# Decay matrices through a DRAM round trip, and a quota that binds only when tiles are scarce

## The chip, the cores and the metric

The kernel runs on one core of one Trainium2 chip. A core has TensorE (PE in the profile), VectorE (DVE), ScalarE (ACT), GpSimd (POOL), SyncE (SP, which here only issues DMAs) and 16 DMA engines. The metric is the device time of one execution in microseconds; the median of several runs counts.

## The reference

Two layers over 256 tokens of width 1024, in float32. Each layer is a SwiGLU FFN (inner width 2816), a mixer, and a second FFN, each with a DeepNorm residual and LayerNorm. Layer 0's mixer is a hybrid of a gated delta rule (GDN, 8 value heads) and a state space scan (SSD, 16 heads); layer 1's is a sparse attention (NSA). What matters here are the decay matrices of the hybrid:

```python
def decay_matrix(cs):
    n = cs.shape[-1]
    mask = np.tril(np.ones((n, n), dtype=bool))
    return jnp.exp(jnp.where(mask, cs[..., :, None] - cs[..., None, :], -jnp.inf))
...
    g_cum = jnp.cumsum(g, axis=-1)                 # gated_delta_rule, one g per token and head
    decay = decay_matrix(g_cum)
    attn = jnp.einsum('bhncd,bhnsd->bhncs', q, k) * decay
...
    a_cs = jnp.cumsum(adt, axis=-1)                # ssd_scan
    seg = decay_matrix(a_cs)
    y_diag = jnp.einsum('bgcls,bgecls,bcsgep->bclgep', cb, seg, xdt)
```

All g are negative, so the cumulative sums fall along the tokens. The kernel works in blocks of 128 tokens, with 24 heads (8 GDN, 16 SSD) side by side. For a head and a block it needs exp(cum[t] - cum[s]) with s on the partitions and t along the row; entries with t < s are masked away later, by the masks that are multiplied into q-k and C-B products.

## The kernel before, in words

The program is written as a list of operations on virtual tiles (class Plan). `Plan.order` then simulates the engines with a price for each operation and writes out one fixed order for all engines, SP among them; `emit` issues it. Every engine works through its part in that order, and waits where an operand isn't there. So a change to any operation may reorder all the others. A `copy` may be given to ACT or to DVE, whichever that order finds free earlier.

Every activation tensor and every split weight is a tile of 128 x 1024 floats with the tag m4; there are 36 of them. A weight is loaded raw (four buffers, tag raw, on SP's queue) and split into a high and a low part: `whi` (a copy with rounding to fp32r, on ACT or DVE) and `wlo` (the remainder, on DVE). A product takes three fp32r matmuls. Tiles belong to streams: W (split weights), M (mixers), S and Z (SSD and gates), L and G (residuals and FFN products), P and Q (attention). `QUOTAS` bounds how many tiles a stream may hold: W has (12, 24). The first number holds as long as a tile of another stream (L and G excepted) which comes earlier in the program has not been given its memory yet (`pending_before`), the second otherwise. The check stands in `try_alloc` inside `Plan.order`.

The hybrid mixer (`hybrid`) computes the z gate of the GDN, then the small logits, from which g comes (tile g24: 128 tokens x 2 blocks x 24 heads), then k and q with their short convolutions (`gdn_conv`, `conv_tile`). The rest is five generators that `weave` interleaves so that PE always finds work: `delta` (the triangular solve of the GDN), `space` (value and SSD projections), `gate` (the SSD's z gate), `space2` (the SSD scan) and `out_a` (the first half of the output projection).

`decays` is called twice in `delta` (tile DT, one for each block) and four times in `space2` (tile G). A call makes the matrices for eight heads. It works on g split into gh + gl: for four heads at a time POOL writes `bm`, which is g of partition r repeated along t and set to zero where t < r (an affine_select for gh and one for gl); PE multiplies both by `m_gtr`, the matrix that is 1 for r > s, into one PSUM bank, which gives the sum of g over s < r <= t; ACT takes Exp out of PSUM into DT or G. So a call has four selects, four matmuls of 128 x 512 and two Exp. In `delta`, DT is then multiplied with bp and the k-k product into AT (8 DVE steps per block), from which the solve starts; bp comes from the squared norms of k, through a power on POOL. In `space2`, G is multiplied by the C-B product and is the stationary operand of eight matmuls.

Of the kernel before, what the change touches and what calls it, by code (L numbers as in the profile page):

```python
# [9 lines left out]
F32 = mybir.dt.float32  # L10
F32R = mybir.dt.float32r
I32 = mybir.dt.int32
AF = mybir.ActivationFunctionType
OP = mybir.AluOpType
# [14 lines left out]
CAPS = {  # L29
    "raw": (RAW, "SB"), "m4": (M4, "SB"), "x": (2, "SB"),  # L30
    "cv": (3, "SB"),
    "ps": (2, "PSUM"), "mp": (2, "PSUM"), "acc": (4, "PSUM"),
}

# [14 lines left out]
def H3(t, h):  # L49
    return t.rearrange("p (h t) -> p h t", h=h)  # L50
# [26 lines left out]
class V:  # L77
# [59 lines left out]
    def to_broadcast(self, shape):  # L137
        return self._new(("bc", list(shape)), np.broadcast_to(self.ids, shape[1:]))

    def bitcast(self, dt):  # L140
        return self._new(("bit", dt), self.ids, dtype=dt)

    def real(self):
        x = self.t.real
        for s in self.chain:
            if s[0] == "get":
                x = x[s[1]]
            elif s[0] == "re":
                x = x.rearrange(s[1], **s[2])
            elif s[0] == "bc":  # L150
                x = x.to_broadcast(s[1])
            else:
                x = x.bitcast(s[1])
        return x
# [7 lines left out]
class Plan:  # L162
# [152 lines left out]
    def order(self, caps):  # L315
# [43 lines left out]
        def try_alloc(key):  # L359
            q = queues[key]  # L360
            while heads[key] < len(q):
                t = q[heads[key]]
                wait = blocked[key].get(id(t))
                if not wait:
                    return
                fs = free_slots[t.tag]
                if not fs:
                    return
                if t.quota is not None:
                    small, big = t.quota  # L370
                    lim = small if pending_before(t.tag, t.stream, t.order) else big
                    if live[key] >= lim:
                        return
                i = min(range(len(fs)), key=lambda j: fs[j])
                t.slot_free = fs.pop(i)
                live[key] += 1
                heads[key] += 1
                del blocked[key][id(t)]
                granted.append(t)
                for op in wait:  # L380
                    op.alloc.remove(t)
                    op.ready = max(op.ready, t.slot_free)
                    if not op.alloc:
                        release_ready(op)
# [147 lines left out]
class K:  # L532
# [43 lines left out]
    def consts(self):  # L576
# [12 lines left out]
        self.m_le = sel("m_le", OP.is_ge, -1, 1)  # L589
        self.m_lt = sel("m_lt", OP.is_gt, -1, 1)  # L590
        self.m_gt = sel("m_gt", OP.is_gt, 1, -1)
        self.m_gtr = self.one([P, P], "m_gtr", F32R)
        self.copy(self.m_gtr, self.m_gt)
        self.mhalf = self.one([P, 1], "mhalf")
        nc.vector.memset(self.mhalf, -0.5)

# [395 lines left out]
        V.tensor_scalar(dst, dst, 1.0, None, OP.add)  # L992
        V.reciprocal(dst, dst)

    def decays(self, g, dst, stream, bank):

        nc = self.nc
        for q in range(2):
            bm = self.m4(1024, "bm", stream, F32R).rearrange("p (e h t) -> p e h t", e=2, h=4)
            for e in range(2):  # L1000
                nc.gpsimd.affine_select(bm[:, e], g[e][:, q * 4:q * 4 + 4, None].to_broadcast([P, 4, P]),
                                        pattern=[[0, 4], [1, P]], compare_op=OP.is_ge, fill=0.0, base=0,
                                        channel_multiplier=-1)
            ps = self.bank(bank)
            for e in range(2):
                nc.tensor.matmul(ps, self.m_gtr, bm[:, e].rearrange("p h t -> p (h t)"), start=e == 0, stop=e == 1)
            nc.scalar.activation(dst[:, q * 4:q * 4 + 4, :], H3(ps, 4), AF.Exp)

    def z_gate(self, x, w_in, c0, zs):

# [21 lines left out]
    def hybrid(self, x, then):  # L1032
# [66 lines left out]
        V.scalar_tensor_tensor(sp, xs, 0.0, sp, OP.max, OP.add)  # L1099
        g = self.sm([P, 2, 24], "g24")  # L1100
        V.scalar_tensor_tensor(g, sp, -1.0, rate[:, None, :].to_broadcast([P, 2, 24]), OP.mult, OP.mult)
        gh, gl = (self.sm([P, 2, 24], n, dtype=F32R) for n in ("gh", "gl"))
        V.tensor_copy(gh, g)
        V.tensor_tensor(gl, g, gh.bitcast(F32), OP.subtract)
        g2 = [gh, gl]
        pg = self.bank("mp")
        gf = g.rearrange("p b h -> p (b h)")
        for n, m in enumerate((self.m_le, self.m_gt, self.ones)):
            nc.tensor.matmul(pg[:, n * 48:(n + 1) * 48], m, gf, start=True, stop=True)
        E = self.sm([P, 3, 2, 24], "E")  # L1110
        nc.scalar.activation(E.rearrange("p a b h -> p (a b h)"), pg[:, :144], AF.Exp)
        eg, ek = E[:, 0], E[:, 1]


        kT = H3(self.m4(1024, "kT"), 4)
# [50 lines left out]
        def delta():  # L1166

            for b in range(2):
                tb = slice(b * P, (b + 1) * P)
                DT = H3(self.m4(1024, f"DT{b}"), 8)  # L1170
                self.decays([t[:, b, 0:8] for t in g2], DT, "M", "acc")
                pk, pq = self.bank("acc"), self.bank("acc")
                for h in range(4):
                    nc.tensor.matmul(pk[:, h * P:(h + 1) * P], kT[:, h, tb], kT[:, h, tb], start=True, stop=True)
# [231 lines left out]
        def space2():  # L1406
# [4 lines left out]
            for q in range(2):  # L1411
# [6 lines left out]
                for b in range(2):  # L1418
# [11 lines left out]
                    V.tensor_tensor(cb, pc[:, :P], self.m_le, OP.mult)  # L1430
                    G = H3(self.m4(1024, "G", "S"), 8)
                    yield
                    self.decays([t[:, b, 8 + q * 8:16 + q * 8] for t in g2], G, "S", "mp")
                    V.tensor_tensor(G, G, cb[:, None, :].to_broadcast([P, 8, P]), OP.mult)
                    yield
                    ps = self.bank("mp")
# [515 lines left out]
def program(tc, ctx, ins, stages):  # L1952
# [3 lines left out]
    order = plan.order({k: n for k, (n, _) in caps.items()})  # L1956
    pools = {}
    for tag, (n, space) in caps.items():
        kw = dict(space=PSUM) if space == "PSUM" else {}
        pools[tag] = (ctx.enter_context(tc.tile_pool(name="t_" + tag, bufs=n, **kw)), n)  # L1960
    plan.emit(tc, pools, order)
    return plan
# [24 lines left out]
```

## Time and profile before

| | |
|---|---|
| median of 3 runs (range) | 1135.66 us (1134.3 to 1138.0) |
| profiled execution, its own time | 1135.04 us |
| its span in the profile, instructions | 1133.3 us, 16526 |
| PE, DVE, ACT, POOL busy | 1114.1, 893.5, 510.3, 64.5 us |
| moved by DMA | 198.38 MB, mean 175 GB/s |
| stretch of the hybrid mixer | about 198 to 420 us |
| stretch of the NSA mixer | about 815 to 940 us |

Nearly all instructions carry the line of the helper that emits them (L508), so groups are told apart by the names of their tiles: `out<-in`. A row of a group ends with the busy time, the mean of one in ns, and the engine's idle time before them with what ended it. PE's rows have a pipelined, modelled end, so two matmul rows overlap; what a matmul takes on PE is read from the distance between starts. Raw loads and other DMAs are issued by SP and appear with the time from issue to landing.

### The profile page before, as it was taken

The numbers are of one execution on the slowest core, as the hardware profiler recorded it, in microseconds if no ns is written. First come the engines' busy times: TensorE is split into PE (matmuls) and PEld (weight loads), VectorE is DVE, ScalarE is ACT, GpSimd is POOL, SyncE is SP. The second block draws the span as 40 slices with busy tenths as digits, with TensorE's granted clock in tenths as the row PEclk, the third lists the DMA queues.
The fourth block names the chain that finished last, engine by engine and source line by source line (L and its number), as shares of the span: only waits on it lengthen the run. The fifth ranks groups of instructions, "written<-read, shape, count | busy, mean of one in ns | idle before, by whom it ended". The sixth has DMA issues, their size and how long they took to land. (4 is left out here: it accounts for less than half of the span.)

```text
span 1133.3 us, 16526 instructions
## 1 busy us (share of the span) xinstructions
PE 1114.1 (98%) x6558; PEld 950.3 (84%) x6558; DVE 893.5 (79%) x1490; ACT 510.3 (45%) x911; POOL 64.5 (6%) x104
## 2 busy tenths in 40 slices
PE   9999999999999999999999999999999999999997
PEld 7888888898999778888888888888877677888886
DVE  8977778789979998777767967776887799777755
ACT  6543332378545655533334634332354656433320
POOL 1000000021011410000000000000000200000000
PEclk9999999999999999999999999999999999999999
DMA  9966552544632275755563765555364136755510
GB/s 337 335 212 209 187 194 88 174 131 126 223 123 75 77 266 177 260 193 181 185 221 112 264 209 185 188 166 176 126 198 137 38 118 224 244 195 186 186 38 37
DMA packets 150743, 198.38 MB, mean 175 GB/s; under 512 B 9453, under 2 KB 127626, under 8 KB 150666
## 3 DMA queue, kind: packets, MB, share of 16 engines
q1 hardware_dynamic: 150666, 197.33, 52.5%
q8 instruction: 51, 0.84, 0.3%
q14 instruction: 26, 0.21, 0.1%
HBM read 194.04 MB, written 1.05 MB: 172 GB/s over the span
## 5 line engine op out<-in xcount | busy, mean ns | idle before, releaser
L508 DVE TENSOR_TENSOR wlo<-raw,whi 128x1024 fp32r<-128x1024 f32 (+1 forms) x349 | 416.3, 1214 | 8.6 <-ACT whi L508 5.8
L508 PE MATMUL ps<-x,whi 128*128 128x512 f32 (+1 forms) x1616 | 378.1, 364 | 0.9 <-ACT cv L508 0.8
L508 PEld LDWEIGHTS ps<-x,whi 128*128 128x128 f32 x1616 | 285.4, 189 | 46.0 <-ACT cv L508 2.0
L508 ACT ACTIVATE whi<-raw 128x1024 fp32r<-128x1024 f32 x255 | 257.0, 1050 | 13.8 <-DMA raw<-in_ffn_w_in_dram 11.6
L508 PE MATMUL acc<-whi,g 128*128 128x512 f32 x704 | 230.7, 391 | 0.0
L508 PE MATMUL ps<-x,wlo 128*128 128x256 f32 x1400 | 227.8, 283 | 1.5 <-DVE wlo L508 1.5
L508 ACT ACTIVATE sg<-ps 128x256 f32<-128x256 f32 x162 | 62.2, 384 | 348.8 <-PE ps L508 348.8
L508 PEld LDWEIGHTS ps<-x,wlo 128*128 128x128 f32 x1400 | 202.7, 190 | 14.1 <-DVE wlo L508 1.7
L508 DVE TENSOR_TENSOR sg<-ps,sg 128x256 f32<-128x256 f32 x162 | 68.7, 424 | 161.7 <-ACT sg L508 161.5
L508 PEld LDWEIGHTS acc<-whi,g 128*128 128x128 f32 x704 | 132.5, 188 | 25.9
L508 PE MATMUL acc<-wlo,g 128*128 128x512 f32 x352 | 138.1, 392 | 0.0
L508 PE MATMUL ps<-whi,x 128*128 128x512 f32 (+1 forms) x480 | 129.9, 387 | 0.5 <-DVE x L508 0.5
L508 PEld LDWEIGHTS ps<-whi,x 128*128 128x128 f32 x480 | 85.9, 188 | 17.2 <-issue 1.3
L508 PEld LDWEIGHTS acc<-wlo,g 128*128 128x128 f32 x352 | 66.4, 189 | 10.9
L508 PE MATMUL ps<-wlo,x 128*128 128x512 f32 (+1 forms) x240 | 68.1, 381 | 0.5 <-DVE wlo L508 0.5
L508 PE MATMUL acc<-whi,x 128*128 128x512 f32 x192 | 63.6, 403 | 0.0
L508 DVE CAST whi<-raw 128x1024 fp32r<-128x1024 f32 (+2 forms) x94 | 63.6, 679 | 0.0
L508 POOL TENSOR_TENSOR lnve<-lnve,mhalf 128x1 f32<-128x1 f32 x12 | 11.5, 955 | 717.1 <-DVE lnve L508 717.1
L508 PEld LDWEIGHTS ps<-wlo,x 128*128 128x128 f32 x240 | 43.2, 188 | 8.2 <-DVE wlo L508 0.9
L508 ACT ACTIVATE sg<-sg 128x256 f32<-128x256 f32 x74 | 30.9, 417 | 34.0 <-DVE sg L508 34.0
L508 PEld LDWEIGHTS acc<-whi,x 128*128 128x128 f32 x192 | 35.6, 188 | 8.4 <-issue 1.8
L508 DVE SCALAR_TENSOR_TENSOR cv<-cv,arena 128x255 f32<-128x255 f32 (+2 forms) x84 | 41.5, 497 | 1.3 <-ACT cv L508 0.6
(253 smaller groups left out, 1011.0 us busy)
## 6 DMA issues: line engine op xcount, KB each, us to landing
raw<-in_ffn_w_in_dram SPq DMA_DIRECT2D x74, 1024.0 KB, 5.1
raw<-in_ffn_w_out_dram SPq DMA_DIRECT2D x44, 1024.0 KB, 5.0
raw<-in_hyb_w_in_dram SPq DMA_DIRECT2D x20, 1024.0 KB, 5.0
raw<-in_ffn_w_in_dram SPq DMA_DIRECT2D x24, 512.0 KB, 4.6
raw<-in_hyb_w_out_dram SPq DMA_DIRECT2D x8, 1024.0 KB, 4.9
raw<-in_nsa_w_in_dram SPq DMA_DIRECT2D x5, 1024.0 KB, 5.0
raw<-in_nsa_w_out_dram SPq DMA_DIRECT2D x4, 1024.0 KB, 4.7
w<-in_nsa_cmp_w_dram SPq DMA_DIRECT2D x8, 512.0 KB, 8.7
```

The costliest lines, as they stand in the source:

```text
L508: r = getattr(getattr(nc, eng), fn)(*[res(a) for a in args], **{k: res(a) for k, a in kw.items()})
```

## The change

Two things change. First, in the hybrid's preparation one more matmul forms the cumulative sums with the heads on the partitions (48 x 128: two blocks of 24 heads); the cumulative sums with the tokens on the partitions, which were already in the PSUM bank, are copied to a tile `cs`. The 48 x 128 matrix is copied out of PSUM (`cT`) and written to a tile in DRAM (`cum`). Each call of `decays` then reads eight rows of `cum` back into DT or G, repeated over all 128 partitions by the access pattern of the DMA (512 KB written to SBUF). ACT forms Relu(cs[s] - cum[t]) for each head (scale -1, the head's column of `cs` as bias), and Exp of its negative for four heads at a time, in place. For t >= s that is exp(cum[t] - cum[s]) as before; for t < s it is 1 instead of what it was, and masked away later. The split of g, the tiles `bm`, the constant `m_gtr`, the selects and the matmuls are gone. `spread` builds the repeating access pattern.

Second, in `try_alloc` the smaller quota holds only when eight or fewer tiles of the tag are free.

```diff
+    "dr": (1, "DRAM"),
...
+    def spread(self, n):
+        v = self._new(("all", n), self.ids)
+        v.n = n
+        return v
...
+            elif s[0] == "all":
+                x = x.partition_broadcast(s[1]).rearrange("p a b -> p (a b)")
...
-                    lim = small if pending_before(t.tag, t.stream, t.order) else big
+                    lim = small if len(fs) <= 8 and pending_before(t.tag, t.stream, t.order) else big
...
-        self.m_gtr = self.one([P, P], "m_gtr", F32R)
-        self.copy(self.m_gtr, self.m_gt)
...
-    def decays(self, g, dst, stream, bank):
+    def decays(self, cum, r0, cs, dst):
         nc = self.nc
+        nc.sync.dma_start(dst.rearrange("p h t -> p (h t)"), cum[r0:r0 + 8, :].spread(P))
         for q in range(2):
-            bm = self.m4(1024, "bm", stream, F32R).rearrange("p (e h t) -> p e h t", e=2, h=4)
-            for e in range(2):
-                nc.gpsimd.affine_select(bm[:, e], g[e][:, q * 4:q * 4 + 4, None].to_broadcast([P, 4, P]),
-                                        pattern=[[0, 4], [1, P]], compare_op=OP.is_ge, fill=0.0, base=0,
-                                        channel_multiplier=-1)
-            ps = self.bank(bank)
-            for e in range(2):
-                nc.tensor.matmul(ps, self.m_gtr, bm[:, e].rearrange("p h t -> p (h t)"), start=e == 0, stop=e == 1)
-            nc.scalar.activation(dst[:, q * 4:q * 4 + 4, :], H3(ps, 4), AF.Exp)
+            for h in range(q * 4, q * 4 + 4):
+                nc.scalar.activation(dst[:, h, :], dst[:, h, :], AF.Relu, scale=-1.0, bias=cs[:, h:h + 1])
+            d = dst[:, q * 4:q * 4 + 4, :]
+            nc.scalar.activation(d, d, AF.Exp, scale=-1.0)
...
-        gh, gl = (self.sm([P, 2, 24], n, dtype=F32R) for n in ("gh", "gl"))
-        V.tensor_copy(gh, g)
-        V.tensor_tensor(gl, g, gh.bitcast(F32), OP.subtract)
-        g2 = [gh, gl]
...
+        nc.tensor.matmul(pg[:48, 384:512], gf, self.m_le, start=True, stop=True)
...
+        cs = self.sm([P, 2, 24], "cs")
+        V.tensor_copy(cs.rearrange("p b h -> p (b h)"), pg[:, :48])
+        cT = self.sm([48, P], "cT")
+        V.tensor_copy(cT, pg[:48, 384:512])
+        cum = self.plan.tile("dr", [48, P], F32, "cum", space="DRAM")
+        nc.sync.dma_start(cum, cT)
...
-                self.decays([t[:, b, 0:8] for t in g2], DT, "M", "acc")
+                self.decays(cum, b * 24, cs[:, b, 0:8], DT)
...
-                    self.decays([t[:, b, 8 + q * 8:16 + q * 8] for t in g2], G, "S", "mp")
+                    self.decays(cum, b * 24 + 8 + q * 8, cs[:, b, hs], G)
```

More of the change, by code (lines that the diff above doesn't have):

```diff
@@ L1958, in program @@
     for tag, (n, space) in caps.items():
-        kw = dict(space=PSUM) if space == "PSUM" else {}
+        kw = dict(space=dict(PSUM=PSUM, DRAM=bass.MemoryType.DRAM)[space]) if space != "SB" else {}
         pools[tag] = (ctx.enter_context(tc.tile_pool(name="t_" + tag, bufs=n, **kw)), n)
```

## The prediction

> **What bounds the kernel now.** I read the page's first two parts and its chain, then the hybrid mixer by stages, then the groups of instructions that the change touches, then the waits.
>
> ```profile
> span 1133.3 us, 16526 instructions
> PE 1114.1 (98%) x6558; PEld 950.3 (84%) x6558; DVE 893.5 (79%) x1490; ACT 510.3 (45%) x911; POOL 64.5 (6%) x104
> PE 16%; DVE 1%; DVEq 0%; issue 0%
> ...
> 198.00:420.00 222.00, 219.40 (x1797) 194.66 (x1796) 201.61 (x397) 127.47 (x206) 35.95 (x48) 1.00 0.45 145
> ...
> 240.00:250.00 10.00, 10.00 (x77) 8.21 (x76) 7.30 (x13) 6.82 (x12) 0.86 (x2) 1.00 0.49 156
> 250.00:260.00 10.00, 9.55 (x68) 8.57 (x67) 9.40 (x23) 8.89 (x15) 6.42 (x5) 1.00 0.18 49
> ...
> 820.00:830.00 10.00, 9.43 (x73) 8.88 (x71) 8.18 (x19) 3.56 (x18) 1.36 (x5) 1.00 0.01 2
> 830.00:840.00 10.00, 8.46 (x55) 8.04 (x55) 9.83 (x20) 6.25 (x26) 0.00 (x0) 0.83 0.60 198
> ```
>
> The columns of the stage rows are: stretch and its length, then busy us of PE, PEld, DVE, ACT and POOL, then granted clock, DMA share and GB/s. PE is busy 98% of the span, and the chain, which is followed back only through the last sixth of it, is PE almost alone. In the hybrid stretch (198 to 420) PE lacks 2.6 us of 222; DVE is at 91%, ACT at 57%, the DMA engines at 45%. So a matmul taken out of that stretch is time taken off the end, as long as DVE and ACT still feed PE. The two last rows are the NSA mixer's start: the only place with a gap above 1 us there that a weight load could cause, and a clock of 0.83.
>
> **The change part by part.** First the six calls of the decays (two in the delta part, four in the SSD part).
>
> ```profile
> L508 POOL TENSOR_SCALAR_AFFINE_SELECT bm<-arena 128x512 fp32r<-128x512 f32 x24 | 22.3, 954 | 129.1 <-PE acc L508 68.1 <-DVE arena L508 39.0 <-PE ps L508 18.0
> L508 PE MATMUL mp<-bm,m_gtr 128*128 128x512 f32 x16 | 5.7, 426 | 0.2
> L508 PE MATMUL acc<-bm,m_gtr 128*128 128x512 f32 x8 | 2.6, 408 | 0.4 <-POOL bm L508 0.4
> L508 PE MATMUL mp<-bm,m_gtr x16: 390/398/499, 337.5 to 402.4; 128*128 128x512 f32 x16
> ...
> 247.07 1.09 PE L508 MATMUL acc<-bm,m_gtr 128*128 128x512 f32 x4
> 248.00 0.38 PE L508 MATMUL acc<-kT 128*128 128x128 f32 x2
> 248.22 0.39 PE L508 MATMUL acc<-qT,kT 128*128 128x128 f32 x2
> ...
> 257.74 0.50 PE L508 MATMUL acc<-bm,m_gtr 128*128 128x512 f32 x1 [0.45 <-POOL bm L508]
> ```
>
> *Matmuls removed.* 16 + 8 = 24. Their busy means (426, 408 ns) overlap the next instruction; what they take on PE is the distance between starts: four of them from 247.07 to 248.00, 0.93 / 4 = 0.232 us. 24 x 0.232 = 5.6 us, all on the path. With them goes the one gap in which PE waited for their input, 0.45 us at 257.74; I take 0.5 us for that and 0.2 us more in the other group. What is late next there is the product of DT with kq, and that has its own cover (below).
>
> *One matmul added*: g transposed and summed, 48 x 128 out. Nearest: a pair of 128x128 f32 records, 248.00 to 248.22, 0.22 us. It uses 48 of the columns, and the order that is planned charges a turn for that; bounds 0.2 to 0.5 us, I take 0.3.
>
> *POOL*: 24 selects, 22.3 us, go. POOL is 6% busy, so this is worth nothing by itself. It shows on DVE, though:
>
> ```profile
> 236.88 3.98 POOL L508 TENSOR_SCALAR_AFFINE_SELECT bm<-arena 128x512 fp32r<-128x512 f32 x4 [38.96 <-DVE arena L508]
> 236.02 0.20 DVE L508 SCALAR_TENSOR_TENSOR arena<-arena 128x48 f32<-128x48 f32 x1
> 237.05 0.64 DVE L508 TENSOR_TENSOR arena<-arena 128x48 fp32r<-128x48 f32 x1
> 240.29 1.12 DVE L508 CAST whi<-raw 128x1024 fp32r<-128x1024 f32 x1
> L508 DVE CAST whi<-raw 128x1024 fp32r<-128x1024 f32 x90 | 61.7, 688 | 0.0
> ```
>
> The first four selects run from 236.9 to 240.9 us; in that time a 128x48 step of DVE takes 0.64 instead of 0.20, a cast 1.12 instead of 0.69. An estimate from these two: about 0.4 us of DVE for each pair of selects, 12 x 0.4 = 5 us off DVE's 201.6. DVE isn't the last wait, so 0 in the sum; it is the cover for what follows.
>
> *DVE steps*: the two that made gh and gl go (0.2 and 0.6 us), two copies out of PSUM come (cs, cT, of the 0.2 us kind). Even; 0.
>
> *ACT*: 12 Exp out of PSUM become 12 Exp in place, and 48 Relu of 128x128 with a bias pointer are new.
>
> ```profile
> L508 ACT ACTIVATE P<-ps,arena 128x128 f32<-128x128 f32 x16 | 5.7, 377 | 2.8 <-DVE arena L508 2.8
> L508 ACT ACTIVATE G<-mp 128x512 f32<-128x512 f32 x8 | 4.7, 598 | 3.4 <-PE mp L508 3.3
> L508 ACT ACTIVATE h<-h 128x512 f32<-128x512 f32 x24 | 15.0, 629 | 2.0 <-PE mp L508 1.8
> 872.52 0.47 ACT L508 ACTIVATE P<-acc,arena 128x256 f32<-128x256 f32 x1 [2.75 <-DVE arena L508]
> 872.90 0.19 ACT L508 ACTIVATION_READ_ACCUMULATOR P<-acc,arena 128x1 f32 x1
> L508 ACT ACT_TABLE_LOAD x22 | 28.2, 1283 | 6.4 <-DMA h<-in_x_dram 3.5 <-DVE cv L508 1.7 <-DMA arena<-in_ssd_a_log_dram 1.0
> ```
>
> An Exp of 128x128 with a bias pointer takes 0.377 us, of which the next instruction overlaps 0.09 (872.52 + 0.47 against 872.90): 0.29. SBUF as source costs 0.03 more (629 against 598): 0.3 us each, 48 x 0.3 = 14.4 us; the Exps 12 x 0.03 = 0.4 us. ACT in 198 to 420 goes from 127.5 to 142 us of 222. Hidden by its 94 us of idle time: 0 in the sum; if that cover were gone, +14.4 us. Whether Relu brings table loads no row of before shows. With a load on either side of each group of four Relu it would be 24 x 1.283 = 31 us more, and ACT at 173 of 222. But only 22 loads stand among ACT's 911 instructions, though copies, squares and scale steps lie between the Silu and the Exp everywhere: I count Relu with these and take 0. [...]
>
> *Transfers*: one of 24 KB to DRAM, six of 512 KB back, each a row of 4 KB read for every partition. The kernel has the same pattern in its LayerNorm rows:
>
> ```profile
> L508 SPq DMA_DIRECT2D lng<-in_ln_g_dram x6: 340/396/504, 159.7 to 1084.5; - x6
> DMA to landing us min/median/max: 3.4/5.4/7.4
> out_dram<-h SPq DMA_DIRECT2D x4, 256.0 KB, 2.1
> SPq L508 <- DVE wlo L508: 106.8, 19, 12.4
> SPq L508 <- DVE cv L508: 31.6, 4, 10.5
> ```
>
> SP issues seven more, 7 x 0.4 = 2.8 us of a queue that in this stretch waits 107 us for DVE's wlo alone. The write waits on SP for DVE's cT, and the reads for the write's landing (2.1 us by the out rows; up to 5.4 by the lng rows); queued behind them on SP are the weights' raw loads, for which ACT's whi waits. Four raw buffers cover 3 us of that. From g (236.2) the first DT then stands at 236.5 + 0.5 + 2.1 to 5.4 + 5.4 = 244.5 to 248, and its Relu and Exp take 8 x 0.3 + 2 x 0.63 = 3.7 us: ready between 248 and 252. It is needed at 258.2 (the first AT step):
>
> ```profile
> 251.87 2.91 POOL L508 TENSOR_TENSOR arena<-arena,mhalf 128x16 f32<-128x16 f32 x1 [11.00 <-DVE arena L508]
> 258.22 2.18 DVE L508 SCALAR_TENSOR_TENSOR AT<-DT,arena,kq 128x128 f32<-128x128 f32 x8
> ```
>
> AT waits for bp, which comes out of the power at 251.87 and the DVE steps behind it, so 6 us or more cover the transfers: 0. If late, each costs up to its landing time, 5.4 us. The G of the SSD part are needed from about 337 us on (the m_gtr row with 16): cum has then been in DRAM for 90 us, and S tiles that bm held are free.
>
> *Copy of m_gt to m_gtr* at the start: 0, PE waits there for x and the first weights.
>
> *The quota.* Split weights could hold 12 tiles while an older tile of another stream waited; now 24 unless at most 8 of 36 are free. It only acts where many tiles are free: by the program's order at the start of the hybrid, where 16 weight tiles of the gate stand beside a handful of others. PE waits nowhere there. In the NSA's start 20 weight tiles and some 13 to 15 others leave fewer than 8, so I expect no effect. Nearest rows for the ends:
>
> ```profile
> PE ps L508 <- DVE wlo L508: 2.0, 2, 1.5
> 831.99 0.38 PE L508 MATMUL ps<-x,wlo 128*128 128x256 f32 x1 [1.53 <-DVE wlo L508]
> ```
>
> Best: that wait goes (1.5), and with it the stretch at clock 0.83, which is 10 x 0.17 = 1.7 us: -3.2. Worst: weights take tiles that the mixers need, and the 2.6 us that PE lacks in the hybrid double: +2.6. I take 0, nearest to the first row, since the wait is where the quota doesn't reach.
>
> **Sum:** -5.6 - 0.5 - 0.2 + 0.3 = -6.0 us. The profiled execution took 1135.04 us, 1.74 more than its span; it lies 0.6 below the median of the runs, 1135.66. 1135.04 - 6.0 = 1129.0, from the median 1129.7; I say 1129.5. With the bounds of the small terms and the shifts that a new order of all instructions brings (some 2 us), its own range is 1127.0 to 1132.0.
>
> **The rivals.**
>
> *ACT becomes the bound of the delta part: slower.* For: between 240 and 260 ACT has 20 - 15.7 = 4.3 us idle, and 16 Relu (4.8 us) want to go there, before conv steps and whi copies that feed PE, all in ACT's order. Price: what of the 14.4 us isn't hidden. From 6.0 us on, 42%, it is no gain; with 9.5 us exposed it is +3.5, 1139. Against: 94 us idle in the stretch, copies that the planned order can give to DVE, and POOL no longer slowing DVE. 1 in 10.
>
> *The transfers eat the gain: same.* Late landings in two of six calls, 2 x 2 to 2 x 3 us, where PE has little else (the first block, and the last G near 400 us): 1133 to 1136. For: SP waits up to 12.4 us at once for wlo. Against: the 6 us of cover. 16 in 100.
>
> *The clock.* The removed matmuls are long dense ones, and where PE gets thinner the granted clock may fall as in the 830 row: 1.7 us for each such fall. One or two in the hybrid give 1131 to 1133. Against: 1.00 in every hybrid row although PE is full of 64x64 pieces there. [...] 6 in 100.
>
> *The quota works in the NSA too.* The 3.2 us above as well: 1126 or so; to 1124 if DVE's 5 us also close part of PE's gaps. 14 in 100. That the quota does nothing at all is part of my forecast.
>
> **Numbers.** Forecast 54 in 100, rivals 10, 16, 6 and 14. A run of this kernel tells changes of about 0.3%, 3.4 us, so 1132.3 and 1139.1 are the lines. Faster: 54 + 14 + half of the clock's 6 = 71. Slower by over 0.3%: the slow rival where more than 9.4 us are exposed, and some of the transfers' tail: 9. Same: 20. The range 1124 to 1137 leaves out about half of the slow rival and the tails of the others.
>
> **What would show it.** Right: no bm and m_gtr rows; PE's count down by about 24 matmuls and its busy sum in the hybrid by 6 to 8 us, with the first instruction of the next FFN about 6 us earlier; 48 Relu near 0.38 us and no more than 22 table loads; six 512 KB reads landing in 4 to 7 us; the NSA and FFN stages as long as before. Wrong: new rows of PE or PEld waiting for ACT G, ACT cv, DVE AT or whi between 240 and 310; raw loads late behind a cum issue on SP; a clock row under 1.00 in the hybrid; or an NSA stage that changed by more than 2 us either way, which would be the quota or the new order.

## The result and the profile after

| | before | after |
|---|---|---|
| median of 4 runs each (range) | 1135.73 us (1134.3 to 1138.0) | 1126.93 us (1126.38 to 1127.89) |
| ratio, 95% interval | | 0.9925 [0.9912, 0.9937] |
| profiled execution, its span | 1135.04, 1133.3 us | 1127.44, 1125.7 us |

The change makes the kernel 8.8 us faster by the medians, 7.6 us by the two profiled executions. First the page after (the span, and the engines' busy time):

```profile
span 1125.7 us, 16509 instructions
PE 1109.0 (99%) x6536; PEld 945.8 (84%) x6536; DVE 875.5 (78%) x1474; ACT 532.5 (47%) x971; POOL 49.1 (4%) x81
PE 93%; DVE 3%; ACT 2%; issue 1%; DMA 1%; POOL 0%; SPq 0%; DVEq 0%; ACTq 0%
```

PE lost 5.1 us of busy time and 22 matmul rows. The chain that ended last (the third line) is PE's for 93% of the span; the chain of before, with its 16% for PE, could be followed only through 17% of the span, so the two shares can't be compared. To see where the 7.6 us come from, the program is cut at two of its LayerNorms, each of which starts with one power on POOL. The first row is after's, right behind the hybrid, the second that of before (the helper's line is L516 in after and L508 in before):

```profile
437.44 0.99 POOL L516 TENSOR_TENSOR lnve<-lnve,mhalf 128x1 f32<-128x1 f32 x1 [9.92 <-DVE lnve L516]
```
```profile
440.93 0.99 POOL L508 TENSOR_TENSOR lnve<-lnve,mhalf 128x1 f32<-128x1 f32 x1 [9.92 <-DVE lnve L508]
```

So the hybrid ends 3.5 us earlier. The same cut at the start of the NSA, 811.4 and 808.0 us, leaves the two FFNs between as they were (370.5 us in both, rounded), and from there to the last LayerNorm it is 316.5 us before and 312.3 after: 4.2 us. The windows of both kernels between these cuts (PE, PEld, DVE, ACT, POOL busy with their instructions, granted clock, DMA share, GB/s), after first:

```profile
0.00:437.40 437.40, 432.64 (x2879) 376.90 (x2880) 359.79 (x636) 244.50 (x412) 24.31 (x47) 0.99 0.58 191
808.00:1120.30 312.30, 305.73 (x1717) 250.55 (x1716) 234.84 (x397) 137.41 (x310) 19.61 (x28) 0.99 0.44 149
...
198.00:420.00 222.00, 219.96 (x1790) 196.94 (x1788) 189.89 (x385) 149.67 (x266) 18.86 (x25) 0.98 0.51 168
820.00:830.00 10.00, 8.90 (x71) 8.43 (x69) 9.18 (x19) 6.41 (x36) 0.00 (x0) 1.00 0.02 6
830.00:840.00 10.00, 9.83 (x71) 6.30 (x75) 6.69 (x12) 3.62 (x8) 1.91 (x1) 1.00 1.04 354
```
```profile
0.00:440.90 440.90, 436.75 (x2901) 379.06 (x2902) 374.45 (x651) 223.25 (x352) 42.39 (x71) 1.00 0.56 183
811.40:1127.90 316.50, 306.88 (x1718) 252.97 (x1716) 238.12 (x398) 137.35 (x311) 16.94 (x26) 0.99 0.43 147
```

In each row the length minus PE's busy time is PE's idle time: up to the end of the hybrid 4.1 us before and 4.8 after. PE's busy time also holds what a halved clock adds. Such a stretch is new in after's hybrid, the 0.98 of the third row; finer windows show it, beside those of a later kernel (pe_back, below), which has none:

```profile
297.90:301.30 3.40, 2.81 (x67) 2.36 (x67) 3.27 (x8) 2.27 (x5) 0.00 (x0) 1.00 0.43 164
301.30:304.70 3.40, 3.40 (x72) 3.40 (x69) 3.29 (x7) 0.10 (x1) 0.00 (x0) 0.51 0.00 0
304.70:308.10 3.40, 3.40 (x21) 3.34 (x19) 1.22 (x3) 1.36 (x2) 0.00 (x0) 0.50 0.82 247
308.10:311.50 3.40, 3.40 (x101) 3.23 (x100) 1.26 (x3) 0.00 (x0) 0.00 (x0) 0.99 0.40 143
```
```profile
297.00:303.80 6.80, 6.80 (x74) 6.26 (x72) 6.70 (x14) 5.91 (x12) 0.00 (x0) 1.00 0.53 161
303.80:310.00 6.20, 6.20 (x142) 5.59 (x139) 5.67 (x11) 2.71 (x6) 0.00 (x0) 1.00 0.66 210
```

From 301.3 to 308.1 after runs at half the clock (0.51 and 0.50): 6.8 us in which, by that clock, 3.4 us of work is done. From start to start, 32 of the solve's pieces (`acc<-Y,XT`) take 1.70 us in it (302.16 to 303.86) and 0.93 behind it (309.48 to 310.41); three matmuls of 128x256 take 0.64 us in it (305.44 to 306.08) and 0.35 in before, at 1.00 (338.54 to 338.89). So I split the time up to a cut into three: PE's *idle* time (length minus busy), the *clock's loss* (half of all stretches at clock 0.5) and the *work* that is left. The clock's loss is an upper bound of what the clock costs, since a wait for another engine inside such a stretch isn't doubled: DVE's wlo took 1.22 us at 303.1, in the stretch, and at 311.9, behind it. The table has all kernels of this study (their changes are told below; each ratio is to runs of before on the same chip, with medians of 1134.4 to 1135.7). Each is split from its own profiled execution, with the hybrid's end as first cut and the part from the NSA's start to the last LayerNorm as the second. The last two columns are from all runs of a kernel: the mean clock granted over an execution, and the median of span times clock, which is the span without the clock's loss:

| kernel | median us | ratio to before | end of hybrid = work + loss + idle | NSA and last FFN = work + loss + idle | clock of its runs, median (range) | span x clock |
|---|---|---|---|---|---|---|
| before | 1135.73 | | 440.9 = 436.8 + 0 + 4.1 | 316.5 = 303.5 + 3.4 + 9.6 | 0.996 (0.994 to 0.999) | 1128.7 |
| after | 1126.93 | 0.9925 [0.9912, 0.9937] | 437.4 = 429.2 + 3.4 + 4.8 | 312.3 = 304.0 + 1.7 + 6.6 | 0.9945 (0.993 to 0.995) | 1119.1 |
| q_only | 1135.68 | 1.0007 [0.9996, 1.0019] | 444.6 = 436.5 + 1.7 + 6.4 | 313.0 = 303.9 + 3.4 + 5.7 | 0.994 (0.992 to 0.998) | 1127.1 |
| d_only | 1133.42 | 0.9989 [0.9978, 1.0000] | 438.8 = 430.9 + 1.7 + 6.2 | 316.2 = 304.5 + 1.7 + 10.0 | 0.992 (0.989 to 0.997) | 1122.8 |
| relu2 | 1134.15 | 0.9998 [0.9982, 1.0014] | 444.1 = 433.0 + 1.7 + 9.4 | 315.0 = 304.3 + 3.4 + 7.3 | 0.9935 (0.989 to 0.998) | 1125.9 |
| min_dve | 1123.41 | 0.9902 [0.9889, 0.9915] | 433.9 = 429.6 + 0 + 4.3 | 311.0 = 304.4 + 0 + 6.6 | 0.997 (0.994 to 0.999) | 1118.3 |
| q_nsa | 1129.81 | 0.9946 [0.9933, 0.9959] | 438.3 = 430.1 + 1.7 + 6.5 | 313.7 = 305.3 + 0 + 8.4 | 0.997 (0.994 to 0.999) | 1124.0 |
| q_hyb | 1133.76 | 0.9985 [0.9973, 0.9997] | 437.0 = 430.6 + 1.7 + 4.7 | 319.1 = 303.2 + 6.8 + 9.1 | 0.991 (0.989 to 0.997) | 1122.0 |
| pe_back | 1125.86 | 0.9915 [0.9902, 0.9928] | 437.3 = 435.4 + 0 + 1.9 | 312.2 = 304.1 + 1.7 + 6.4 | 0.998 (0.996 to 0.999) | 1121.9 |
| min_old | 1131.07 | 0.9962 [0.9949, 0.9974] | 435.7 = 428.6 + 0 + 7.1 | 313.6 = 304.8 + 0 + 8.8 | 0.997 (0.997 to 0.999) | 1126.3 |
| pool_back | 1132.60 | 0.9979 [0.9968, 0.9991] | 443.9 = 430.6 + 5.1 + 8.2 | 313.7 = 303.9 + 3.4 + 6.4 | 0.993 (0.989 to 0.996) | 1123.4 |
| min_q4 | 1131.65 | 0.9974 [0.9965, 0.9984] | 439.8 = 431.0 + 3.4 + 5.4 | 314.0 = 305.4 + 0 + 8.6 | 0.995 (0.991 to 0.997) | 1124.7 |
| warm7 | 1136.65 | 1.0019 [1.0008, 1.0029] | 445.8 = 430.3 + 3.4 + 12.1 | 314.0 = 302.6 + 3.4 + 8.0 | 0.991 (0.988 to 0.992) | 1125.0 |
| min_warm | 1138.35 | 1.0036 [1.0023, 1.0049] | 448.5 = 431.5 + 6.9 + 10.1 | 312.6 = 302.0 + 3.4 + 7.2 | 0.990 (0.989 to 0.993) | 1126.7 |

The split is rough (PE's ends are modelled, some rows may be missing, one execution stands for each kernel). For it speaks that the second part's work, which no change touches, comes out between 302.0 and 305.4 in all kernels, while q_hyb's busy time reads 310.0. These 3.4 us are also the size below which I don't trust a difference of work.

The loss belongs to an execution as much as to a kernel. With one and the same order d_only's eleven runs go from 1130.48 us at clock 0.997 to 1136.68 us at 0.989, pool_back's twelve from 1130.85 at 0.996 to 1137.19 at 0.989. So a stretch at half clock that stands in one kernel's trace and not in another's is not by itself a difference between the kernels; the clocks of all runs have to be compared. Nor is all of the loss time: d_only's runs lie 6.2 us apart where their losses (1 - clock, times the span) lie 9.1 apart. And 2.6 us of it in after, 1.7 in before, fall into the last 5.4 us of the span, behind the last LayerNorm, where PE has no work left (clock 0.52 and 0.69, PE busy for 0.00).

### The profile page after: what moved, and what is told of

The parts are those of the page before. It is cut to its first block, busy times and chain, and to the rows that moved or that the text cites. A ratio compares the mean times of both kernels' runs of the same rounds, so it can differ in the third digit from the quotient of the medians.

```text
span 1125.7 us, 16509 instructions
## 1 busy us (share of the span) xinstructions
PE 1109.0 (99%) x6536; PEld 945.8 (84%) x6536; DVE 875.5 (78%) x1474; ACT 532.5 (47%) x971; POOL 49.1 (4%) x81
## 4 chain that ended last, share of the span: by engine, by line
PE 93%; DVE 3%; ACT 2%; issue 1%; DMA 1%; POOL 0%; SPq 0%; DVEq 0%; ACTq 0%
PE ps L516 56%; PE acc L516 32%; PE mp L516 5%; ACT P L516 1%; DVE qs L516 1%; DMA raw<-in_ffn_w_in_dram 1%; DVE wlo L516 0%; POOL arena L516 0%; DVE arena L516 0%; SPq L516 0%; DVE o L516 0%; DVE x L516 0%; ACT Y L516 0%; DVE h L516 0%; DVE XT L516 0%
## 5 line engine op out<-in xcount | busy, mean ns | idle before, releaser
L516 DVE TENSOR_TENSOR wlo<-raw,whi 128x1024 fp32r<-128x1024 f32 (+1 forms) x349 | 415.7, 1212 | 11.3 <-ACT whi L516 8.2
L516 PE MATMUL ps<-x,whi 128*128 128x512 f32 (+1 forms) x1616 | 379.2, 364 | 0.8 <-ACT ktok L516 0.7
L516 PEld LDWEIGHTS ps<-x,whi 128*128 128x128 f32 x1616 | 285.7, 189 | 45.9 <-ACT cv L516 1.2
L516 ACT ACTIVATE whi<-raw 128x1024 fp32r<-128x1024 f32 x265 | 266.5, 1047 | 10.8 <-DMA raw<-in_ffn_w_in_dram 9.4
L516 PE MATMUL acc<-whi,g 128*128 128x512 f32 x704 | 230.6, 391 | 0.0
L516 ACT ACTIVATE sg<-ps 128x256 f32<-128x256 f32 x162 | 62.2, 384 | 351.9 <-PE ps L516 351.9
L516 PE MATMUL ps<-x,wlo 128*128 128x256 f32 x1400 | 227.4, 283 | 0.0
L516 PEld LDWEIGHTS ps<-x,wlo 128*128 128x128 f32 x1400 | 202.5, 190 | 12.2 <-issue 0.8
L516 DVE TENSOR_TENSOR sg<-ps,sg 128x256 f32<-128x256 f32 x162 | 68.7, 424 | 162.5 <-ACT sg L516 162.3
L516 PEld LDWEIGHTS acc<-whi,g 128*128 128x128 f32 x704 | 132.5, 188 | 25.9
L516 PE MATMUL acc<-wlo,g 128*128 128x512 f32 x352 | 138.1, 392 | 0.0
L516 PE MATMUL ps<-whi,x 128*128 128x512 f32 (+1 forms) x480 | 130.2, 387 | 1.3 <-DVE whi L516 1.0
L516 PEld LDWEIGHTS ps<-whi,x 128*128 128x128 f32 x480 | 85.7, 188 | 19.0 <-DVE whi L516 1.8
L516 PEld LDWEIGHTS acc<-wlo,g 128*128 128x128 f32 x352 | 66.4, 189 | 10.9
L516 PE MATMUL ps<-wlo,x 128*128 128x512 f32 (+1 forms) x240 | 68.1, 382 | 0.6 <-DVE wlo L516 0.5
L516 PE MATMUL acc<-whi,x 128*128 128x512 f32 x192 | 64.3, 402 | 0.0
L516 DVE CAST whi<-raw 128x1024 fp32r<-128x1024 f32 (+2 forms) x84 | 56.9, 680 | 0.5 <-DMA raw<-in_ffn_w_in_dram 0.5
L516 PEld LDWEIGHTS ps<-wlo,x 128*128 128x128 f32 x240 | 43.2, 188 | 8.2 <-DVE wlo L516 1.5
L516 ACT ACTIVATE sg<-sg 128x256 f32<-128x256 f32 x74 | 30.9, 418 | 33.9 <-DVE sg L516 33.9
L516 DVE SCALAR_TENSOR_TENSOR cv<-cv,arena 128x255 f32<-128x255 f32 (+2 forms) x84 | 39.6, 476 | 8.1 <-ACT cv L516 7.5
L516 POOL TENSOR_TENSOR lnve<-lnve,mhalf 128x1 f32<-128x1 f32 x12 | 11.5, 956 | 726.9 <-DVE lnve L516 726.9
L516 PEld LDWEIGHTS acc<-whi,x 128*128 128x128 f32 x192 | 35.7, 189 | 7.3 <-issue 0.7
```

Source lines behind the costliest of these rows:

```text
L516: r = getattr(getattr(nc, eng), fn)(*[res(a) for a in args], **{k: res(a) for k, a in kw.items()})
```

## The experiments

**The two parts alone.** The theory: the decays give the gain, and the quota nothing. The rival: the quota works in the NSA. q_only is before with the line of the quota, d_only is after without it:

```diff
-                    lim = small if pending_before(t.tag, t.stream, t.order) else big
+                    lim = small if len(fs) <= 8 and pending_before(t.tag, t.stream, t.order) else big
```

> The kernel before with the quota line alone. Stages are read from the starts of the LayerNorm powers on GpSimd (before: 196.9, 440.9, 811.4, 947.9 us; after: 198.6, 437.4, 808.0, 939.2). Theory A (the quota made the NSA stage 5.3 us shorter: 136.5 to 131.2 us between the sixth and the tenth... that is 811.4 to 947.9): this run shows an NSA of 130 to 132 us, a hybrid of 243 to 245 us as before, about 1130.5 us in all. Theory B (no edit owns the NSA's gain; any change to the program shuffles the NSA's order by some us): NSA anywhere from 130 to 139 us, and the total 1130 to 1138 us. Theory C (forecast on record: the quota does nothing): NSA 136 to 137 us and 1135 to 1136 us.

> The changed kernel with the old quota line, so the decays alone. Forecast on record: the hybrid stage shorter by 6 us, 238 us against 244.0, if no clock window falls in it, and the NSA as before. Theory A: hybrid 238 to 241 us, NSA 136 to 137 us, 1129.5 to 1132 us. Theory B: hybrid 238 to 241 us, NSA anywhere from 130 to 139 us, total 1124 to 1134 us.

Measured: 1.0007 and 0.9989, both nothing that can be told from no change. Neither part alone makes the 8.8 us, and both totals lie above what theory A gave them. In q_only the NSA did come out at 131.3 us, as theory A had it, but the hybrid grew. The table says where the rest is: q_only gains 3.5 us behind the NSA's start and loses 3.7 before it (2.3 more idle, 1.7 by the clock), d_only gains 2.1 in the hybrid and 0.3 behind. The runs add what the one trace hides: d_only's clock is lower, in seven of its eleven runs below any of before's, and without the loss its span is 5.9 us shorter than that of before (q_only's 1.6, after's 9.6). Its one run at clock 0.997 took 1130.48 us, those of before at 0.997 on the same chip 1133.5 to 1134.6. So the decays alone saved 3 to 6 us, and a lower clock took most of it back.

The wait that the prediction left at its place is the plain sign of the quota. It is the NSA's first 256-column projection; d_only has it, q_only and after have only a shorter one on ACT near that place:

```profile
829.91 0.38 PE L516 MATMUL ps<-x,wlo 128*128 128x256 f32 x1 [1.53 <-DVE wlo L516]
```
```profile
837.12 0.51 PE L508 MATMUL ps<-x,whi 128*128 128x256 f32 x2 [0.66 <-ACT ktok L508]
```
```profile
829.95 0.51 PE L516 MATMUL ps<-x,whi 128*128 128x256 f32 x2 [0.66 <-ACT ktok L516]
```

**The quota by stage.** q_nsa is after with the new rule only for tiles from the NSA on, q_hyb with it only for those before (`nsa0` is the program place where the NSA starts):

```diff
-                    lim = small if len(fs) <= 8 and pending_before(t.tag, t.stream, t.order) else big
+                    lim = small if (len(fs) <= 8 or t.order < self.nsa0) and pending_before(t.tag, t.stream, t.order) else big   # q_nsa
+                    lim = small if (len(fs) <= 8 or t.order >= self.nsa0) and pending_before(t.tag, t.stream, t.order) else big  # q_hyb
```

> The changed kernel with the new quota rule only for tiles of the NSA mixer and later ones. Theory A (the quota removes the NSA's wait of 1.53 us for a wlo at its first 256-column projection, and a half-clock window behind it): hybrid as with the decays alone (first two stages end near 438.8 us), that wait gone, NSA and last FFN together 312 to 313.5 us against 316.5 before, total 1129 to 1130.5 us. Theory B (the NSA is shuffled by anything): NSA and last FFN 311 to 317 us with no tie to the wait.

> The changed kernel with the new quota rule only for tiles before the NSA mixer. Theory A: the hybrid as in the changed kernel (first two stages end near 437.4 us, with or without half-clock windows), the 1.53 us wait in the NSA back, NSA and last FFN together 315.5 to 317 us, total 1130 to 1131.5 us. Theory B: NSA and last FFN anywhere from 311 to 317 us.

Measured: q_nsa 0.9946, without the wait, in the range of theory A; q_hyb 0.9985, with the wait of 1.53 us again (at 828.08), but 2.3 us above the range, with 6.8 us of the clock's loss in the NSA. So the rule acts in the NSA. Over all kernels: PE's idle time in the second part is 9.6, 10.0, 9.1 and 8.8 us with the old rule there (before, d_only, q_hyb, min_old), and 5.7 to 8.4 us, mean 6.8, in the seven with the new rule at its threshold of 8 and the planner as it was. That is 2.6 us for the quota, of which the wait is 1.5, less the 0.7 of the new one (these kernels share parts of their order, so they are not seven independent measurements). The clock's loss there isn't tied to the rule: 3.4, 1.7, 6.8, 0 with the old, 1.7, 3.4, 3.4, 0, 0, 1.7, 3.4 with the new.

**ACT: twice the Relu, and none.** The theory: ACT's new work is hidden. relu2 does each Relu a second time on its own result, which changes no value; min_dve gives the step to DVE, as the smaller of cum[t] - cum[s] and 0:

```diff
+            for h in range(q * 4, q * 4 + 4):                                                # relu2
+                nc.scalar.activation(dst[:, h, :], dst[:, h, :], AF.Relu, scale=1.0, bias=self.zcol)
...
-                nc.scalar.activation(dst[:, h, :], dst[:, h, :], AF.Relu, scale=-1.0, bias=cs[:, h:h + 1])
+                nc.vector.tensor_scalar(dst[:, h, :], dst[:, h, :], cs[:, h:h + 1], 0.0, OP.subtract, OP.min)   # min_dve
-            nc.scalar.activation(d, d, AF.Exp, scale=-1.0)
+            nc.scalar.activation(d, d, AF.Exp)
```

> The changed kernel with each Relu of the decays done twice (the second changes no value): 48 more activations, 14 to 18 us more on ScalarE in the hybrid. If the added ScalarE work is hidden, as forecast, the hybrid stage stays at 238.8 us within 2 us. If ScalarE binds the delta part (the slow rival), a good part of 14 us appears there: hybrid 243 us or more, the total 1131 us or more.

> The changed kernel with the Relu on VectorE instead: 48 tensor_scalar (subtract, then min with 0) and Exp with scale 1. VectorE gets 48 x about 0.25 us = 12 us, ScalarE loses 48 x 0.39 = 18.7 us of busy time. If neither engine binds the hybrid: within 2 us of the changed kernel, 1125 to 1129 us. If ScalarE binds: 1 to 4 us faster. If VectorE binds: 3 us or more slower.

Measured: relu2 1134.15 us, 7.2 above after; min_dve 1123.41, the fastest kernel here. The 48 new Relu keep ACT busy for 15.2 us (0.39 each, but they overlap). The order made room by moving nine whi casts to DVE, so ACT's total rose only by 5.0 us and DVE's by 9.7. It cost relu2 4.6 us of PE's idle time in the hybrid and 3.8 us that the split calls work; the clock's loss is 5.1 us in both kernels. More work on ACT, and on DVE in its place, is not free there. min_dve in two windows:

```profile
0.00:433.90 433.90, 429.64 (x2879) 374.29 (x2880) 366.89 (x682) 236.11 (x368) 22.78 (x48) 1.00 0.58 193
198.00:420.00 222.00, 220.38 (x1810) 197.63 (x1809) 200.05 (x434) 139.00 (x220) 17.30 (x25) 1.00 0.52 172
```

ACT has 10.7 us less than in after and DVE 10.2 us more, and the hybrid is 3.5 us shorter: in this execution, the quickest of min_dve's four, there is no half clock (1.00), and idle time is about as in after. Against before it is 7.0 us shorter, all of it work. Its interval touches that of after (0.9915 and 0.9912); by the medians it is 3.5 us better, but without the clock's loss only 0.8 (1118.3 against 1119.1). That ACT's Relu cost after anything is therefore not shown.

> The decays with the VectorE min, and the old quota rule. Theory A: NSA and last FFN 315.5 to 317 us with the wait of 1.53 us, against 311.0 with the new rule; the hybrid within 2 us of 235 us as long as no half-clock window falls in it: 1127 to 1130 us. If the new rule is needed in the hybrid as well (the decays alone gave 241.1 us with one half-clock window, the quota alone 246.2), the hybrid is 238 us or more here and the total 1131 us or more.

min_old is min_dve with the old quota: 1131.07 us, 7.7 more, with the 1.53 us wait at 829.31 again, 2.2 us more idle in the second part and 2.8 in the hybrid, and 373.1 instead of 370.5 us for the two FFNs between. So the rule is worth as much with the faster decays, and not in the NSA alone; why the FFNs between grew is open.

**The matmuls put back.** pe_back is after with 24 matmuls of 128 x 512 that nobody reads, four in each call, held until the call's transfer has been issued (and, not shown below, a few copies at the start that make their operands). If each is worth 0.232 us, it must be slower by 5.6:

```diff
+        with _Gate(self.plan, len(self.plan.ops) - 1):
+            for q in range(2):
+                ps = self.bank("mp")
+                for e in range(2):
+                    nc.tensor.matmul(ps, self.m_gtr, self.fill, start=e == 0, stop=e == 1)
```

> The changed kernel with four idle matmuls of 128x512 put back into each call of the decays (24 in all, from constants into a PSUM bank that nothing reads, released by the call's transfer). If the 5.6 us of TensorE time are what the decays gained, this run is 5 to 6 us slower than the changed kernel, 1132 to 1133 us, unless the dense matmuls spare it the half-clock windows at 301 to 308 us (then down to 1129 us). If the removed waits and the freed VectorE were the gain, it stays within 2 us, 1125 to 1129 us.

Measured: 1125.86 us, not slower at all, and the hybrid ends at 437.3 as in after. Read by the end alone, this says that the removed matmuls were worth nothing. Its window says something else:

```profile
0.00:437.30 437.30, 435.38 (x2903) 379.24 (x2904) 360.59 (x637) 246.57 (x418) 21.34 (x47) 1.00 0.59 191
```

PE has 24 instructions more and is idle 1.9 instead of 4.8 us, with no half clock: 6.2 more work, 3.4 less loss, 2.9 less idle. By this split the matmuls cost about what was forecast, and PE lost as much less elsewhere. The clock's part is no chance of one trace: the five runs of pe_back have 0.996 to 0.999, the four of after 0.993 to 0.995. Without the loss pe_back is 2.8 us longer than after; that the rest of the 5.6 went into the shorter idle time fits this one trace. Over the table the work up to the hybrid's end is 435.4 to 436.8 us in the three kernels with these matmuls (mean 436.2) and 428.6 to 433.0 in the eleven without (mean 430.5): 5.7 us for 24 matmuls. This reading came after the result; the total alone fits the expectation's last branch, that the gain was not the matmuls' time. What isn't separated: whether it is their density or the other order of all instructions that kept the clock up.

**The selects put back.** pool_back is after with the 24 selects on POOL, read by nobody. PE, DVE, ACT and SP have the same instructions in the same order as in after:

```diff
+        with _Gate(self.plan, len(self.plan.ops) - 1):
+            for n in range(4):
+                nc.gpsimd.affine_select(self.fill.rearrange("p (h t) -> p h t", h=4), cs[:, n:n + 4, None].to_broadcast([P, 4, P]),
+                                        pattern=[[0, 4], [1, P]], compare_op=OP.is_ge, fill=0.0, base=0,
+                                        channel_multiplier=-1)
```

> The changed kernel with four idle selects of 128x512 put back on GpSimd in each call of the decays (24 in all, into a buffer that nothing reads), released by the call's transfer. If selects slow VectorE as read from the trace of before (0.4 us for a pair), VectorE's busy time in 198 to 420 us rises by 4 to 6 us over 189.9; if VectorE's load is what gave the hybrid 3.6 us with the matmuls put back, the total goes to 1129 to 1131 us; if VectorE is only a cover, it stays within 2 us of 1126.9 us.

Measured: 1132.60 us, 5.7 above after, and 4.3 without the clock's loss. DVE's busy time from 198 to 420 rose only by 1.2 us (189.9 to 191.1), but that window holds 378 of its instructions instead of 385, since all is later. Up to the hybrid's end the 636 instructions are the same ones, and take 367.14 us instead of 359.79 (after's row is the first of the windows above):

```profile
0.00:443.90 443.90, 435.68 (x2879) 378.92 (x2880) 367.14 (x636) 243.92 (x412) 43.30 (x72) 0.99 0.58 189
```

These 7.3 us for 24 selects are 0.6 us for a pair, where the prediction had 0.4. How they reach PE shows at one place, from the timelines (start, us, engine, what; in brackets the idle time before and who ended it), pool_back first, then the same steps in after:

```profile
255.79 3.10 POOL L516 TENSOR_SCALAR_AFFINE_SELECT fill<-arena 128x512 fp32r<-128x512 f32 x4
258.31 4.46 DVE L516 SCALAR_TENSOR_TENSOR AT<-DT,arena,kq 128x128 f32<-128x128 f32 x8
259.35 2.75 POOL L516 TENSOR_SCALAR_AFFINE_SELECT fill<-arena 128x512 fp32r<-128x512 f32 x4
262.81 2.61 ACT L516 ACTIVATE sw<-AT 32x256 f32<-32x256 f32 x4 [3.75 <-DVE AT L516]
265.88 0.80 PE L516 MATMUL ps<-x,whi 128*128 128x256 f32 x2 [3.14 <-ACT cv L516]
```
```profile
257.19 2.18 DVE L516 SCALAR_TENSOR_TENSOR AT<-DT,arena,kq 128x128 f32<-128x128 f32 x8
259.40 2.74 ACT L516 ACTIVATE sw<-AT 32x256 f32<-32x256 f32 x4 [0.44 <-DVE AT L516]
262.60 0.30 PEld L516 LDWEIGHTS ps<-x,whi 128*128 128x128 f32 x2 [0.41 <-ACT cv L516]
262.60 0.50 PE L516 MATMUL ps<-x,whi 128*128 128x256 f32 x2
```

While the selects run, the eight AT steps take 4.46 instead of 2.18 us. ACT stands in its order before a copy of AT, for 3.75 us, and behind it stands a conv step that PE waits for: 3.14 us, where in after only the weight load waits, 0.41 us, and PE not at all. Then the clock falls, as pool_back's windows show:

```profile
262.40:265.80 3.40, 0.33 (x2) 0.00 (x0) 3.40 (x8) 2.93 (x5) 0.00 (x0) 1.00 0.00 0
265.80:269.20 3.40, 3.32 (x15) 3.33 (x16) 3.40 (x11) 3.20 (x7) 0.00 (x0) 0.50 0.00 0
```

So 2.3 us more on an engine that isn't the bound became 3.1 us more on the one that is, and in this execution up to 1.7 us by the clock; a second fall of 6.8 us at 306.7 stands where after has its own at 301.3. This prices selects beside AT, not those of before: there they ran at 236.9 to 240.9 and 254.7 to 258.3 us, just ahead of AT at 258.2.

**Trying to keep the clock up.** The planner puts dense matmuls first where too few were planned in the last 3.4 us; the number is `KEEP_WARM`. warm7 is after, min_warm min_dve, with 7000 instead of 5500; min_q4 is min_dve with a threshold of 4 tiles in the quota's line:

```diff
-KEEP_WARM = 5500
+KEEP_WARM = 7000                                             # warm7, min_warm
-                    lim = small if len(fs) <= 8 and pending_before(t.tag, t.stream, t.order) else big
+                    lim = small if len(fs) <= 4 and pending_before(t.tag, t.stream, t.order) else big   # min_q4
```

> The changed kernel with KEEP_WARM 7000 instead of 5500, so that the planned order reaches for dense matmuls sooner. If the half-clock windows (6.8 us at 301 to 308, 3.4 us at 875 in the changed kernel) cost half their length each, and go, the first two stages end near 434 us (437.4 before) and the total is 1121.5 to 1124 us. If the time lost there is the delta chain's own (DVE steps between its small matmuls) and the clock only shows it, it stays at 1125.5 to 1128 us. If the windows don't go, the run says nothing on it.

> The decays with the VectorE min (1123.4 us, no half-clock window in the mixers), new quota, KEEP_WARM 7000. There is no window to win back: 1122 to 1125 us. A larger loss would say that the dense-first order itself costs time.

> The decays with the VectorE min, and the small quota only when four or fewer tiles are free. If weights then take tiles that the mixers need, the hybrid or the NSA gets 2 us or more longer (1125.5 us or more); if weights are still what is late, 1121 to 1123 us; if eight was not binding, 1122.5 to 1124.5 us.

Measured: 1136.65, 1138.35 and 1131.65 us, worse by 9.7, 14.9 and 8.2 than the kernels they start from. With dense matmuls first the half clock stands near the hybrid's end: in warm7 the clock is 1.00 from 198 to 420 us and 0.99 from 198 to 445.8, with 3.4 us of loss; in min_warm it is 0.99 from 198 to 425 and 0.97 to 448.5, with 6.9. Why it stands there is not shown. In warm7 PE also waits for a late G, and that wait begins with the transfer: ACT waited 3.2 us for the read of G, DVE for ACT, PE for DVE (us in all, times, longest):

```profile
PEld mp L516 <- DVE G L516: 6.1, 2, 5.1
PE mp L516 <- DVE G L516: 4.9, 2, 4.2
ACT G L516 <- DMA G<-cum: 5.6, 2, 3.2
```

Neither tells what the half clock costs by itself, since the order's own waits came with it (idle 12.1 and 10.1 us). min_q4 took the first branch of its expectation: the hybrid is 5.9 us longer than in min_dve, 3.4 of it the clock's loss, and the second part 2.9. Which tiles came late there stays open.

## Why the prediction was right in its total and wrong in its split

The forecast of 1129.5 is 2.6 us above the measured median of 1126.93. That lies in the whole range of 1124 to 1137, and just under the forecast's own, 1127.0 to 1132.0. The split was -6.0 in the hybrid and 0 elsewhere; it came as -3.5 and -4.2. That the total came so near is in part luck: a gain priced at nothing stood in for one that half failed to arrive. Two of the prediction's own signs of being wrong are there, a clock row under 1.00 in the hybrid (0.98) and a changed NSA, and PE's busy time up to the hybrid's end fell by 4.1 us, not by 6 to 8.

*24 matmuls at 0.232 us, -5.6.* Right as work: 5.7 us over the table, 7.6 between before and after. Wrong as time off the end: the step "a matmul taken out is time taken off" counted PE's idle time as a constant. After lost 3.4 us of it to the clock and 0.7 to idle time. That is what the *rival of the clock* told, which had 6 in 100: two falls of up to 1.7 us, as priced, though the total it forecast (1131 to 1133) did not come, and whether the missing matmuls brought them is not separated from the new order. With no fall, in the one trace of min_dve, the hybrid gained 7.0; and d_only shows the same exchange over all its runs, 5.9 us shorter without the loss and 1.2 with it.

*The quota, 0.* The failed step: "20 weight tiles and some 13 to 15 others leave fewer than 8". Had that held throughout, the rule could not have acted there, and q_nsa shows that it did. The wait of 1.53 us went with the rule in the NSA, and PE's idle time fell by 3.0 us, the clock's loss by 1.7, against 0.5 more work. The rival *the quota works in the NSA too* happened, with its priced -3.2 for the wait and the clock against -4.2 in all. The clock's share is not the rule's (min_old has no loss there, q_only as much as before), and one execution of each kernel can't tell whether it is this order's; that the idle time fell by more than the wait is shown, but by which steps is open.

*POOL's selects, 0.* The size for DVE was about right: 0.6 us for a pair in pool_back, against 0.4. The step from there to 0, "DVE isn't the last wait", is what fails in pool_back: its DVE time went on through ACT's order to PE, 5.7 us in all. That before paid such a price too, and so that taking the selects out gained it, isn't shown.

*ACT, hidden.* Half right. The rows of after, by form (min/median/max in ns, first and last start):

```profile
L516 ACT ACTIVATE DT<-DT,arena x16: 384/387/389, 248.0 to 257.4; 128x128 f32<-128x128 f32 x16
L516 DVE SCALAR_TENSOR_TENSOR AT<-DT,arena,kq x16: 338/341/343, 257.2 to 264.6; 128x128 f32<-128x128 f32 x16
L516 ACT ACTIVATE G<-G,arena x32: 386/392/402, 339.3 to 406.1; 128x128 f32<-128x128 f32 x32
L516 ACT ACT_TABLE_LOAD x20 | 25.7, 1283 | 8.4 <-DVE arena L516 3.6 <-DMA h<-in_x_dram 3.6 <-DMA arena<-in_ssd_a_log_dram 0.9
```

The Relu is the 0.38 us of the forecast, and the 48 keep ACT busy for 15.3 us, near the forecast's 14.4. But ACT's total went up by 22 us (149.7 from 127.5), because the order also gave ACT casts that DVE had before: 81 of whi on DVE instead of 90, which is 9.2 us more on ACT. DVE has 11.7 us less in that stretch, where the forecast had 5. There are 20 table loads instead of 22 (min_dve, without Relu, has 22, and so has pe_back, with it), so Relu brought none here. Total cover of 94 us doesn't make such work free: relu2 paid 7.2 us for 15.2 more. So the mechanism of the slow rival is real. That it acted in after isn't shown: min_dve, where ACT has 10.7 us less, gained 3.5, of which the clock's loss is 2.7.

*The transfers, hidden.* Right for PE. The last G, one of the two places that the rival of the transfers named, is late for ACT (3.0 us of waiting, at 403.5), but PE has other work there; in warm7 it has not. The queue's rows in after, with the time to landing of the read behind each:

```profile
L516 SPq DMA_DIRECT2D cum<-arena x1: 335/335/335, 237.8 to 237.8; - x1
L516 SPq DMA_DIRECT2D DT<-cum x2: 325/338/350, 239.3 to 241.0; - x2
DMA to landing us min/median/max: 3.7/3.7/3.7
L516 SPq DMA_DIRECT2D G<-cum x4: 338/459/497, 332.2 to 397.7; - x4
DMA to landing us min/median/max: 5.4/5.7/5.8
```

The first read is issued 1.5 us after the write, and lands at 243, before the 244.5 to 248 of the forecast; Relu starts at 248.0, AT at 257.2, 1 us earlier than before.

## What to carry to other kernels

Where an engine is 98% busy, split its time into work, idle time and the clock's loss before you believe a change in the total, and compare the clocks of all runs and not of one profile each: here 5.7 us of removed work stood out over fourteen kernels, while idle time and loss together lay anywhere between 1.9 and 17.0 us up to the same cut, since one planner orders everything anew with every edit. "Hidden by idle time" has to be argued at the instructions that stand behind the new one in its engine's order, not from the stretch's total. And a part that alone shows no change (both did here) may still hold half of the gain.

## What the hardware did that I had not expected

*The clock falls also where PE is mostly busy.* The prediction tied it to thin stretches. relu2 does so, with PE busy for 1.3 of the 3.4 us ahead:

```profile
279.50:282.90 3.40, 1.32 (x8) 0.69 (x6) 3.40 (x11) 1.95 (x4) 0.00 (x0) 1.00 0.00 0
282.90:286.30 3.40, 3.26 (x15) 3.26 (x16) 3.40 (x11) 1.36 (x2) 0.00 (x0) 0.50 0.56 154
```

But after's fall at 301.3 follows 2.81 busy us of 3.4, and goes on through a second 3.4 us, with PE busy in all of the first (pool_back's at 306.7 reads just so, behind 2.81 of 3.4). PE runs the solve's small pieces there, as the timeline shows (pieces of 64x64, 64 x 32 results):

```profile
300.83 1.52 PE L516 MATMUL acc<-XT,Y 64*64 64x32 f32 x32 [0.59 <-DVE XT L516]
302.16 1.91 PE L516 MATMUL acc<-Y,XT 64*64 64x32 f32 x32
```

So one fall follows 3.4 us in which PE was busy for 83%, and wholly busy 3.4 us in it did not end it. Nor does the busy share alone decide: in the same trace PE was busy for only 2.40 us from 379.9 to 383.3, and the clock stayed at 1.00 there and in the 3.4 us behind. What else decides, no run here isolates.

*The falls stand on a grid.* In after, before and pool_back the starts of half-clock stretches lie whole multiples of 3.413 us apart: in after 301.3, 874.8 and 1120.5, 168 and 240 of them behind the first; in before 833.0, 880.8 and 1130.0, 14 and 87; in pool_back 265.8 and 306.7, 12. The fall at 833.0 lasts 3.4 us, after's first twice that. Where the grid begins differs from trace to trace: counted from the span's start, the falls lie 1.0 us past a whole multiple in after, 0.1 in before and 2.9 in pool_back. Whether it also differs between executions of one kernel isn't shown, since no kernel has two traces, and why the clock differs between runs of one order isn't either.

*DVE is slowed beside POOL's selects.* The AT step took up to 0.781 us in pool_back, where selects run beside it, and 0.343 at most in after. What makes it longer is not shown.
